# A two-layer hybrid mixer step: the running sum of its branches kept in DRAM, low weight parts made from SBUF, and four conditioning chunks moved into attention

## The chip, the cores and the metric

The kernel runs on one core of one Trainium2 chip. The metric is device time in microseconds (us). TensorE (PE) multiplies, VectorE (DVE) and ScalarE (ACT) work element by element, GpSimd (POOL) does some elementwise work and issues the DMAs that add to what is already at their destination, and SyncE (SP) issues most other DMAs. Each engine runs its own queue of instructions in order and waits on semaphores.

## The reference, cut to what matters

Two layers work on 128 context tokens and 512 latent tokens, 640 in all, with a model width of 1024 in float32. Each layer is

```python
def trunk_layer(x, cond, p, latent, k_ctx, v_ctx):
    mod = jax.nn.silu(cond) @ p['w_ada'] + p['b_ada']
    shift, scale, gate = jnp.split(mod, 3, axis=-1)
    h = rms_norm(x, p['norm_g']) * (1.0 + scale) + shift
    y, k, v = parallel_mixer(h, p, latent, k_ctx, v_ctx)
    return x + gate * y, k, v

    # parallel_mixer: u = h @ p['w_in'] (1024 x 11264), then four branches of u:
    ya = (conformer_conv(...) * jax.nn.silu(a_gate)) @ p['wo_conv']
    yb = (hyena(...) * jax.nn.silu(b_gate)) @ p['wo_hyena']
    yc = (multiscale_pool(...) * jax.nn.silu(c_gate)) @ p['wo_pool']
    yd = (attention(...) * jax.nn.silu(d_gate)) @ p['wo_attn']
    gm = jax.nn.sigmoid(g_merge).reshape(B, L, N_BRANCH, D_MODEL)
    merged = gm[:, :, 0] * ya + gm[:, :, 1] * yb + gm[:, :, 2] * yc + gm[:, :, 3] * yd
    return merged @ p['w_out'], k, v
```

## The kernel before

**Products in three passes.** To keep float32 accuracy with the fast fp32r matmul, every operand is split into a high part and a low part, and each product is high times high, low activation times high weight, and high activation times low weight. `weights()` prepares one weight tile of 128 x 1024: SP loads it as `raw`, ACT casts it to `whi`, ACT writes minus `whi` into `wlo`, and POOL issues a DMA that reads the same weight from DRAM a second time and adds it to `wlo`. (Before the variable `pooled` is set, DVE subtracts instead.) There are two `raw` buffers and three pairs of `whi` and `wlo`. In a tile's 48 matmuls of 320 columns the 16 with `whi` come before the 8 with `wlo`, once for each half (320 tokens) of the activations.

**The order of work.** The Python program runs some generators ("threads") under a planner, the class `Loom`, which decides when each thread may put its next matmuls into PE's queue. It knows estimated costs and latencies, but not when a DMA lands. PE runs exactly that order. The other engines' queues are ordered by a scheduler, with a head start for `weights()`.

**Memory.** Large tiles live in 13 slots of 128 x 2632 floats. Smaller rings hold tiles `t` (3), `u` (4) and `k` (4).

**One layer.** `layers()` does the input projections for Hyena, the attention, and then four calls of `merge()`, one for each branch, each with eight output blocks `d`: a gate projection into the tile `th`, the branch's output projection, and `th` times it. The first call (Hyena) stores `th` in DRAM (`mscr`). `reload()` brings all eight blocks back into two slots (`merged`) during the attention; the calls for attention and pool ("mid") add `th` there with DVE, and the last one (conv) adds and splits the sum. `out_proj()` multiplies with `w_out`, adds the residual, and lets `turned()` (transposes) and `modulated()` (norm, scale, split) make the next layer's input, the two halves of tokens one after the other.

**Conditioning.** `ada_chunk()` multiplies a chunk of `w_ada` (1024 x 256) with the two conditioning vectors: two loads of 512 KB into a `whi` and a `wlo` buffer, 8 matmuls of 256 columns, one copy on ACT (`k<-ax`), and for a gate chunk a store to `grow`. There are 24 chunks: 8 for the first layer at the start, 12 spread over its first stages with a pause of 14 us, and the last 4, the second layer's gates, at lowest priority while the first layer's `out_proj` runs.

**Hyena's tables.** `tables()` loads 1.25 MB into a slot; the second layer's filters are made during the first layer's pool stage, their spectra are kept in DRAM, and the table's slot stays occupied until the second layer's Hyena is done.

Of the kernel before, what the change touches and what calls it, by code (L numbers as in the profile page):

```python
# [10 lines left out]
F32R = mybir.dt.float32r  # L11
# [14 lines left out]
    0, 1024, 1536, 3072, 3584, 4096, 4608, 5632, 5888, 6144, 7168)  # L26
R_DW, R_DWB, R_LNG, R_LNB, R_SW, R_SB, R_SK, R_PS, R_NG, R_BA, NROW = 0, 31, 32, 33, 34, 43, 46, 48, 49, 51, 55
SLOT = 2632
NSLOT = 13
NRAW = 2  # L30
NHI = 3
DORD = "0f4xt15gh2637"
PT = 6.5
# [1 line left out]
HW = 80  # L35
HA = 40
PL = 1
GS = 40.0
EACH = 0.003
ORD = "01456237vkq"  # L40
WAHEAD = 120
# [191 lines left out]
def hybrid_flow_backbone(ctx: ExitStack, tc: tile.TileContext, i, o):  # L233
# [49 lines left out]
    def slot(dt=F32):  # L283
        yield lambda: 0.0 if free else INF
        return Slot(dt)
# [47 lines left out]
    def weights(src, kk, n):  # L333
        yield from wr.get()
        lm.bg = True
        with tc.high_priority(offset=WAHEAD):
            raw = wp.tile([P, 1024], F32, tag="raw", name=nm("raw"), bufs=NRAW)
            hi = wp.tile([P, 1024], F32R, tag="whi", name=nm("whi"), bufs=NHI)
            lo = wp.tile([P, 1024], F32R, tag="wlo", name=nm("wlo"), bufs=NHI)
            w = kk * n  # L340
            rv = raw[:, 0:w]
            sp.dma_start(out=rv.rearrange("p (k c) -> p k c", k=kk), in_=src)
            act.copy(hi[:, 0:w], rv)
            if pooled[0]:

                act.activation(out=lo[:, 0:w], in_=r32(hi[:, 0:w]), func=AF.Copy, scale=-1.0)
                nc.gpsimd.dma_start(out=lo[:, 0:w].rearrange("p (k c) -> p k c", k=kk), in_=src.bitcast(F32R),  # L347
                                    accum_op=ALU.add)
            else:
                dve.tensor_tensor(out=lo[:, 0:w], in0=rv, in1=r32(hi[:, 0:w]), op=ALU.subtract)  # L350
        lm.bg = False
        return (hi[:, 0:w].rearrange("p (k c) -> p k c", k=kk),
                lo[:, 0:w].rearrange("p (k c) -> p k c", k=kk))
# [355 lines left out]
    def ada_later(jobs, step, start):  # L709
        yield lm.pe + start  # L710
        for l, j in jobs:
            yield from ada_chunk(l, j)
            if 4 <= j < 8:
                ada_finish(l, j - 4)
            yield lm.pe + step
# [130 lines left out]
        tr.put()  # L846


    def merge(l, b, ga, nk, wo, merged, mode, ma=None, wait=None):


        for d in range(8):
            if mode == "last" and d % 4 == 0:
                for part in (ma.hi, ma.lo):
                    part.append((yield from slot(F32R)))
            th = yield from tr.get(T)

            def gate(j, ps):
                act.activation(out=th[:, 320 * j:320 * j + 320], in_=ps, func=AF.Tanh, scale=0.5)

            yield from in_proj(l, C_GM + b * D + 128 * d, gate)
            if wait is not None:
                yield wait
            w = yield from weights(wo[:, 128 * d:128 * d + 128].rearrange("(k p) c -> p k c", p=P), nk, 128)
            def take(j, ps):
                tj = th[:, 320 * j:320 * j + 320]
                dve.scalar_tensor_tensor(out=tj, in0=tj, scalar=1.0, in1=ps, op0=ALU.add, op1=ALU.mult)

            yield from both(w, 0, ga, nk, take)
            wr.put(WD)  # L870
            if mode == "first":
                sp.dma_start(out=mscr[l, d], in_=th)
                lm.cur.t += 2.5
            else:
                yield lambda: 0.0 if len(merged) == 2 else INF
                mv = merged[d // 4].v((d % 4) * T, T)
                dve.tensor_tensor(out=mv, in0=mv, in1=th, op=ALU.add)
                if mode == "last":
                    split(ma.h(d), ma.l(d), mv, 0.5)
            tr.put()  # L880

    hT = [None]
# [3 lines left out]
    class Hyena:  # L886
# [32 lines left out]
        def filters(self, q):  # L919
# [115 lines left out]
            if self.nf == 2:  # L1035
                self.Bf.free()
                if early:
                    self.fs.free()
                    self.flt = {}

        def spectra(self):

            yield lambda: 0.0 if self.nf == 2 else INF
            for c in range(4):
                yield lambda: 0.0 if c < 2 or c in self.bu else INF
                self.flt[c] = yield from slot()
                for q in range(2):
                    self.ev_f[c, q].t = load(self.flt[c].v(1280 * q, 1280), spec[c, q])
# [178 lines left out]
    class Attention:  # L1227
        def __init__(self, l):
            self.l = l
            self.gD = [None, None]  # L1230
            self.sT, self.qT, self.rq, self.qv, self.den = {}, {}, {}, {}, {}
            self.ev_kv, self.ev_s, self.ev_v, self.ev_room, self.ev_gd = (Event(lm) for _ in range(5))
            self.ev_q = [Event(lm) for _ in range(4)]
            self.ev_p = [Event(lm) for _ in range(4)]
            self.nq = [0] * 4
            self.nk = 0
            self.hi, self.lo = [], []
            self.pairs, self.ev_pair = [], []
# [359 lines left out]
        def parts(self):  # L1598

            yield self.ev_s  # L1600
            for c in range(8):
                if c % 4 == 0:
                    self.hi.append((yield from slot(F32R)))
                    self.lo.append((yield from slot(F32R)))
                if c == 4:
                    self.ev_room.set()
                yield self.done[c]
                split(self.hi[c // 4].v((c % 4) * T, T), self.lo[c // 4].v((c % 4) * T, T),
                      self.gD[c // 4].v((c % 4) * T, T), 0.5)
# [281 lines left out]
    def layers():  # L1891
# [3 lines left out]
        for l in range(DEPTH):  # L1895
# [37 lines left out]
            lm.spawn(at.values_out(), 0, LATV)  # L1933
            lm.spawn(at.run(), 5.5)
            lm.spawn(at.parts(), 4)
            yield hy.ev_done
            yield from merge(l, 1, hy.gb, 4, i["wo_hyena"][l], None, "first")
            hy.gb.free()
            cv = Conv(l)
            cv.at = at  # L1940
            yield from cv.inputs(range(4))

            merged = []
            lm.spawn(reload(l, merged, at.ev_room), 5)
            gd = Act(at.hi, at.lo)
            lm.spawn(cv.taps(), -1)
            po = Pooling(l)
# [1 line left out]
            po.at = at  # L1949
            lm.spawn(po.windows(), -3)  # L1950
            lm.spawn(cv.norm(), -2, LATN)
            yield from merge(l, 3, gd, 8, i["wo_attn"][l], merged, "mid", None, at.ev_gd)
            gd.free()

            yield from po.gated()
            if l + 1 < DEPTH:
                hys[l + 1].after = cv.ev_norm
                for q in range(2):
                    lm.spawn(hys[l + 1].filters(q), PF0 + q / 10)
            yield from merge(l, 2, po.pa, 4, i["wo_pool"][l], merged, "mid")  # L1960
            po.pa.free()

            yield from cv.gated()
            ma = Act([], [])
            rows = yield from gate_rows(l)
            yield from merge(l, 0, cv.ga, 4, i["wo_conv"][l], merged, "last", ma)
            cv.ga.free()
            hT[0].free()
            for s in merged:
                s.free()  # L1970
            xs = yield from slots(2)
            if l == 0:
                load_x(xs, i["x_prompt"][0], i["x_sample"][0])
            else:
                load_x(xs, scratch[0:LP], scratch[LP:T])
            ssq = sm.tile([P, 5, 4], F32, tag="ssq", name=nm("ssq"))
            if l + 1 < DEPTH:
                lm.spawn(ada_later([(1, j) for j in range(8, 12)], 0.0, GS), 50, LATA)
            if l + 1 < DEPTH:
                xT = yield from slots(2)  # L1980
                evs = [[Event(lm) for _ in range(2)] for _ in range(4)]
# [12 lines left out]
                for x in xs:  # L1994
                    x.free()

    def reload(l, merged, ev):

        yield ev
        for h in range(2):  # L2000
            s = yield from slot()
            load(s.v(0, 4, T), mscr[l, 4 * h:4 * h + 4].rearrange("d p t -> p d t"))
            merged.append(s)

    ev_prm, ev_cond, ev_ssq = Event(lm), Event(lm), Event(lm)
    ev_hdn = [Event(lm) for _ in range(DEPTH)]
    ev_mod = [[Event(lm) for _ in range(4)] for _ in range(DEPTH)]
# [9 lines left out]
    t_hid, t_prm = [0.0], [0.0]  # L2017
    small = load_hidden(s_hid) + [(sel, i["c_sel"], t_prm)] + load_params(s_prm) + [(edge, i["c_edge"], t_prm)]
    chunks = []
    spare = ["whi", "wlo"] * 3 + ["raw"] * 2  # L2020
    h0 = hys[0]
    xs0 = [Slot(), Slot()]

# [138 lines left out]
```

## Time and profile before

| | us |
|---|---|
| median of the runs shown (3) | 2272.85 |
| their lowest and highest | 2267.57, 2273.87 |
| time of the profiled execution | 2271.39 |
| its span, first to last instruction | 2269.6 |
| PE busy in the span | 2189.7 |
| DVE, ACT, POOL busy in the span | 1329.2, 1190.8, 585.5 |

1.8 us of the profiled execution lie outside its span. The profile gives the clock that TensorE was granted as a share of full speed; its mean is 0.992 here. Matmuls are pipelined, so the durations of neighbouring rows overlap, and a stretch's speed is read from start to start.

### The profile page before, as it was taken

The page shows a single profiled execution, that of the slowest core. Times are in us where ns is not written, and L with a number is a line of the kernel's source. Part 1 is how long each engine was busy: PE and PEld are TensorE (multiplying, and loading weights), DVE is VectorE, ACT ScalarE, POOL GpSimd, SP SyncE. Part 2 cuts the span into 40 slices and gives each one's busy share as a digit, 9 for nine tenths or more (in the row PEclk, how much of TensorE's full clock was granted, in tenths as well). Part 3 has the DMA queues.
Part 4 walks back from the last instruction along what each step waited for, and adds up shares of the span by engine and source line. Part 5 has one row for each costly group of instructions (what it writes and reads, how often), then busy time and mean ns, then how long its engine had stood idle before and what let it go on. Part 6 is the DMA issues. An engine that isn't in the chain of part 4 may idle for free. (4 is left out here: it accounts for less than half of the span.)

```text
span 2269.6 us, 40007 instructions
## 1 busy us (share of the span) xinstructions
PE 2189.7 (96%) x15951; PEld 2140.5 (94%) x15951; DVE 1329.2 (59%) x2791; ACT 1190.8 (52%) x2179; POOL 585.5 (26%) x451
## 2 busy tenths in 40 slices
PE   5999999999999999999997999999999999999999
PEld 3899999999999998999996999999999999999999
DVE  5676786656679945443224677855764899612222
ACT  5544457667664345444445544656676543544442
POOL 1744321111012222554211333111111122222221
PEclk9899999999999999999998999999999999999999
DMA  8476775545568879778898865555466698698986
GB/s 277 110 156 137 156 159 114 97 95 99 106 122 147 149 126 182 154 164 161 150 220 239 154 118 120 110 102 101 84 110 118 126 155 150 120 162 148 174 171 138
DMA packets 510536, 322.33 MB, mean 142 GB/s; under 512 B 13016, under 2 KB 499608, under 8 KB 510093
## 3 DMA queue, kind: packets, MB, share of 16 engines
q0 software_dynamic: 223856, 122.96, 42.7%
q1 hardware_dynamic: 285780, 196.68, 28.6%
q8 instruction: 125, 2.05, 0.4%
q14 instruction: 62, 0.51, 0.1%
q10 hardware_dynamic: 713, 0.14, 0.0%
HBM read 302.26 MB, written 17.47 MB: 141 GB/s over the span
## 5 line engine op out<-in xcount | busy, mean ns | idle before, releaser
L193 PE MATMUL mm<-sl,whi 128*128 128x320 f32 x6304 | 1059.1, 313 | 10.6 <-DVE t L178 3.2
L193 PEld LDWEIGHTS mm<-sl,whi 128*128 128x128 f32 x6304 | 951.2, 189 | 18.2 <-DVE sl L178 4.3
L193 PE MATMUL mm<-sl,wlo 128*128 128x320 f32 x3152 | 555.1, 312 | 5.7 <-DMA wlo<-in_w_in_dram 5.7
L347 POOL DMA_DIRECT2D wlo<-in_w_in_dram x173 | 264.4, 1532 | 915.6 <-ACT wlo L178 689.5
L193 PEld LDWEIGHTS mm<-sl,wlo 128*128 128x128 f32 x3152 | 484.0, 189 | 7.4 <-DMA wlo<-in_w_in_dram 6.7
L178 ACT CAST whi<-raw 128x1024 fp32r<-128x1024 f32 (+2 forms) x272 | 255.3, 939 | 429.4 <-PE mm L193 405.1
L178 ACT ACTIVATE wlo<-whi 128x1024 fp32r<-128x1024 f32 (+2 forms) x269 | 254.9, 948 | 29.6 <-PE mm L193 25.7
L178 DVE SCALAR_TENSOR_TENSOR t<-t,mm 128x320 f32<-128x320 f32 x192 | 93.0, 485 | 294.1 <-PE mm L193 244.4
L193 PE MATMUL mm<-whi,sl 128*128 128x256 f32 x1600 | 226.2, 284 | 2.5 <-ACT u L178 1.5
L178 DVE SCALAR_TENSOR_TENSOR sc<-sl,prm,sc 128x640 f32<-128x640 f32 (+14 forms) x232 | 207.3, 893 | 11.4 <-ACT sc L178 6.7
L193 PE MATMUL sc<-sl,sl 128*128 128x128 f32 (+1 forms) x1344 | 203.4, 293 | 5.7 <-DVE u L178 2.8
L193 PEld LDWEIGHTS mm<-whi,sl 128*128 128x128 f32 x1600 | 203.3, 188 | 4.8 <-ACT u L178 1.7
L178 DVE TENSOR_TENSOR h<-ax,h 128x512 fp32r<-128x512 f32 (+1 forms) x200 | 120.1, 604 | 118.7 <-ACT h L178 117.5
L193 PEld LDWEIGHTS sc<-sl,sl 128*128 128x128 f32 x1344 | 179.5, 194 | 8.0 <-DVE u L178 4.0
L178 ACT ACTIVATE t<-mm 128x320 f32<-128x320 f32 x208 | 90.0, 433 | 137.8 <-PE mm L193 135.1
L178 DVE TENSOR_SCALAR_CACHE_REDUCE u<-sc,rq 128x640 f32<-128x640 f32 x128 | 112.6, 880 | 46.2 <-PE sc L193 45.2
L178 ACT ACTIVATE u<-u,nb 128x640 f32<-128x640 f32 x128 | 106.2, 830 | 52.3 <-DVE u L178 51.6
L178 ACT CAST h<-ax 128x512 fp32r<-128x512 f32 (+1 forms) x200 | 102.5, 515 | 55.8 <-PE ax L202 53.6
L193 PE MATMUL mm<-wlo,sl 128*128 128x256 f32 x800 | 126.7, 281 | 4.4 <-DMA wlo<-in_w_in_dram 4.4
L193 PE MATMUL ax<-h,sl 128*128 128x256 f32 (+1 forms) x656 | 120.7, 295 | 4.0 <-DVE h L178 2.7
L202 PE MATMUL ax<-ident,u 128*128 128x128 f32 x752 | 118.5, 273 | 4.7 <-DVE h L178 2.6
L193 PEld LDWEIGHTS mm<-wlo,sl 128*128 128x128 f32 x800 | 108.3, 188 | 5.0 <-DMA wlo<-in_w_in_dram 5.0
(211 smaller groups left out, 2225.9 us busy)
## 6 DMA issues: line engine op xcount, KB each, us to landing
raw<-in_w_in_dram SPq DMA_DIRECT2D x176, 512.0 KB
wlo<-in_w_in_dram POOLq DMA_DIRECT2D x173, 512.0 KB, 6.6
wlo<-in_w_ada_dram SPq DMA_DIRECT2D x19, 512.0 KB
whi<-in_w_ada_dram SPq DMA_DIRECT2D x19, 512.0 KB
raw<-in_wo_attn_dram SPq DMA_DIRECT2D x16, 512.0 KB
wlo<-in_wo_attn_dram POOLq DMA_DIRECT2D x16, 512.0 KB, 6.4
raw<-in_w_out_dram SPq DMA_DIRECT2D x16, 512.0 KB
wlo<-in_w_out_dram POOLq DMA_DIRECT2D x16, 512.0 KB, 6.0
```

The lines of the kernel that those rows point to most:

```text
L178: r = f(*args, **kw)
L193: r = self.real.matmul(out, lhsT, rhs, **kw)
L202: r = self.real.transpose(out, in_, ident)
L347: nc.gpsimd.dma_start(out=lo[:, 0:w].rearrange("p (k c) -> p k c", k=kk), in_=src.bitcast(F32R), accum_op=ALU.add)
```

## The change

- In `weights()`, the DMA that adds to `wlo` reads the tile `raw` in SBUF and not the weight in DRAM: 128 runs of up to 4 KB where it had up to 1024 runs of 512 B. `raw` is thus in use until that DMA has landed, and there are four `raw` buffers.
- There are 12 slots and not 13.
- The two "mid" merges add `th` to `mscr` in DRAM by a DMA on POOL's queue (32 DMAs of 320 KB in all). `reload()` and its two slots are gone; the last merge loads one block of the sum at a time into a tile `u` (16 loads of 320 KB on SP's queue).
- The second layer's four gate chunks run in its own attention, with the pause of 14 us, and not at the end of the first layer.
- Hyena's table slot is freed when the second layer's filters are made, and the table is loaded again at the start of the second layer.
- At the start, two more of the first chunks' halves go to `raw` buffers.

```diff
-NSLOT = 13
-NRAW = 2
+NSLOT = 12
+NRAW = 4
...
                 act.activation(out=lo[:, 0:w], in_=r32(hi[:, 0:w]), func=AF.Copy, scale=-1.0)
-                nc.gpsimd.dma_start(out=lo[:, 0:w].rearrange("p (k c) -> p k c", k=kk), in_=src.bitcast(F32R),
-                                    accum_op=ALU.add)
+                nc.gpsimd.dma_start(out=r32(lo[:, 0:w]), in_=rv, accum_op=ALU.add)
...
+            if mode == "last":
+                mv = yield from ur.get(T)
+                now = load(mv, mscr[l, d])
             th = yield from tr.get(T)
...
             if mode == "first":
                 sp.dma_start(out=mscr[l, d], in_=th)
                 lm.cur.t += 2.5
+            elif mode == "mid":
+                nc.gpsimd.dma_start(out=mscr[l, d], in_=th, accum_op=ALU.add)
+                lm.cur.t += 5.0
             else:
-                yield lambda: 0.0 if len(merged) == 2 else INF
-                mv = merged[d // 4].v((d % 4) * T, T)
+                lm.cur.t = max(lm.cur.t, now)
                 dve.tensor_tensor(out=mv, in0=mv, in1=th, op=ALU.add)
-                if mode == "last":
-                    split(ma.h(d), ma.l(d), mv, 0.5)
+                split(ma.h(d), ma.l(d), mv, 0.5)
+                ur.put()
...
                 if early:
                     self.fs.free()
+                    self.tabE.free()
...
             yield lambda: 0.0 if self.nf == 2 else INF
+            self.tables((yield from slot()))
...
             lm.spawn(at.parts(), 4)
+            if l:
+                lm.spawn(ada_later([(1, j) for j in range(8, 12)], ASTEP, 0.0), 5, LATA)
...
-            merged = []
-            lm.spawn(reload(l, merged, at.ev_room), 5)
...
-            if l + 1 < DEPTH:
-                lm.spawn(ada_later([(1, j) for j in range(8, 12)], 0.0, GS), 50, LATA)
...
-    spare = ["whi", "wlo"] * 3 + ["raw"] * 2
+    spare = ["whi", "wlo"] * 3 + ["raw"] * 4
```

The change moves instructions on every engine. Three places matter for what follows.

On PE, the end of the first layer. The rows with `cs` are the gate chunks (`whi` and `wlo` hold halves of `w_ada`), those with `ident` are transposes of the residual, and the last rows are the first matmuls of the second layer's first `w_in` tile. Before:

```order
L193 MATMUL ax_13052<-whi_13035,cs 32x256 x4
L193 MATMUL ax_13052<-wlo_13037,cs 32x256 x4
L202 MATMUL mm_13073<-ident,sl_12254 128x128 x2
L202 MATMUL mm_13077<-ident,sl_12254 128x128 x2
L193 MATMUL ax_13088<-whi_13084,cs 32x256 x4
L193 MATMUL ax_13088<-wlo_13086,cs 32x256 x4
L193 MATMUL ax_13110<-whi_13106,cs 32x256 x4
L193 MATMUL ax_13110<-wlo_13108,cs 32x256 x4
L193 MATMUL mm_13176<-sl_12262,whi_13160 128x320
L193 MATMUL mm_13176<-sl_12264,whi_13160 128x320
```

Now:

```order
L201 MATMUL mm_13038<-ident,sl_12267 128x128 x2
L201 MATMUL ax_13042<-ident,sl_12267 128x128
L201 MATMUL mm_13057<-ident,sl_12267 128x128 x2
L201 MATMUL mm_13061<-ident,sl_12267 128x128 x2
L192 MATMUL mm_13102<-sl_12275,whi_13089 128x320
L192 MATMUL mm_13102<-sl_12277,whi_13089 128x320
```

The four chunks are gone from between the last transposes and the second layer's first matmuls; the other matmuls of this place stand in the same order.

On ACT, the same place. `k<-ax` are the chunks' copies, `sl<-u` makes high parts of the second layer's input, `sl<-mm` and `sl<-ax` read transposes, and `whi<-raw`, `wlo<-whi` prepare `w_in` tiles. Before, the first two tiles of the second layer are prepared together, after the third chunk's place:

```order
L178 ACTIVATE sl_12261<-mm_13025,mod_1705 128x256
L178 COPY k_13081<-ax_13052 128x256
L178 ACTIVATE sl_12261<-ax_13032,mod_1705 128x128
L178 ACTIVATE sl_12262<-u_13039,mod_1705 128x128
L178 ACTIVATE sl_12262<-u_13039,mod_1705 128x192
L178 CAST whi_13160<-raw_13159 128x1024
L178 CAST whi_13170<-raw_13169 128x1024
L178 ACTIVATE wlo_13161<-whi_13160 128x1024
L178 ACTIVATE wlo_13171<-whi_13170 128x1024
L178 ACTIVATE sl_12261<-mm_13045,mod_1705 128x256
```

Now the first tile's low part (`wlo<-whi`) stands ahead of the norm's row (`t<-ax`, 128 x 384) and the second tile's two parts right behind it; `o` are squares of the residual:

```order
L177 ACTIVATE wlo_13090<-whi_13089 128x1024
L177 ACTIVATE o_12794,ssq_12272<-sl_12267 128x256
L177 ACTIVATE o_12852,ssq_12272<-sl_12267 128x256
L177 ACTIVATE o_12906,ssq_12272<-sl_12267 128x256
L177 ACTIVATE o_12908,ssq_12272<-sl_12267 128x256
L177 COPY t_12279<-ax_12959 128x384
L177 CAST whi_13096<-raw_13095 128x1024
L177 ACTIVATE sl_12275<-u_12964,mod_1708 128x128
L177 ACTIVATE wlo_13097<-whi_13096 128x1024
L177 ACTIVATE sl_12275<-u_12964,mod_1708 128x192
```

What moved is the preparation of these two tiles: from the middle of the input's conversion to its beginning.

On SP, the second layer's attention. `whi<-in_w_ada` and `wlo<-in_w_ada` are a gate chunk's loads and `raw` is a weight tile's. Before, the queue holds weight loads and the first merge's stores at this place:

```order
L342 DMA raw_16070<-in_w_in_dram 128x8x128
L872 DMA mscr<-t_15518 128x640
L342 DMA raw_16216<-in_wo_hyena_dram 128x4x128
L342 DMA raw_16278<-in_w_in_dram 128x8x128
L872 DMA mscr<-t_15699 128x640
L342 DMA raw_16416<-in_w_in_dram 128x4x256
```

Now a chunk's two loads stand behind loads of weight tiles, which wait in turn until a `raw` buffer's low part has landed:

```order
L341 DMA raw_15433<-in_w_in_dram 128x8x128
L341 DMA raw_15597<-in_wo_hyena_dram 128x4x128
L656 DMA whi_15238<-in_w_ada_dram 128x4x256
L656 DMA wlo_15240<-in_w_ada_dram 128x4x256
L1350 DMA out_dram<-sl_14812 128x256
L341 DMA raw_15685<-in_w_in_dram 128x8x128
L341 DMA raw_15842<-in_wo_hyena_dram 128x4x128
L341 DMA raw_15904<-in_w_in_dram 128x8x128
L656 DMA whi_15505<-in_w_ada_dram 128x4x256
L656 DMA wlo_15507<-in_w_ada_dram 128x4x256
```

Four such pairs of loads have come into this stretch, in order behind the weights' own.

## Rows read from the trace of the kernel before

**Rows 1.** The page of the whole execution: its span, and TensorE's busy time.

```profile
span 2269.6 us, 40007 instructions
...
PE 2189.7 (96%) x15951; PEld 2140.5 (94%) x15951; DVE 1329.2 (59%) x2791; ACT 1190.8 (52%) x2179; POOL 585.5 (26%) x451
```

**Rows 2.** Who PE waited for, whole span: us in total, times, longest us.

```profile
PE mm L193 <- DMA wlo<-in_w_in_dram: 10.1, 6, 2.9
PE ax L193 <- DMA wlo<-in_w_ada_dram: 7.6, 4, 3.8
PE ax L193 <- DMA whi<-in_w_ada_dram: 1.6, 3, 0.9
```

**Rows 3.** Stretches of 10 us: length, PE busy, granted clock, DMA share, GB/s.

```profile
1200.00:1210.00 10.00, 8.56 (x79) 1.00 0.22 67
1210.00:1220.00 10.00, 5.00 (x62) 0.99 1.01 327
1220.00:1230.00 10.00, 7.30 (x32) 0.67 1.05 230
1230.00:1240.00 10.00, 7.71 (x33) 0.67 1.26 247
1240.00:1250.00 10.00, 9.24 (x58) 0.99 0.77 209
...
2120.00:2130.00 10.00, 10.00 (x70) 1.00 1.11 250
```

**Rows 4.** PE in order of time around the layer boundary; idle before a row in brackets.

```profile
1207.28 1.10 PE L193 MATMUL mm<-wlo,sl 128*128 128x256 f32 x8
...
1209.40 0.64 PE L193 MATMUL ax<-whi,cs 128*32 128x256 f32 x8
...
1209.86 0.61 PE L193 MATMUL ax<-wlo,cs 128*32 128x256 f32 x8
...
1214.17 0.64 PE L193 MATMUL ax<-wlo,cs 128*32 128x256 f32 x8 [2.32 <-DMA wlo<-in_w_ada_dram]
...
1221.04 4.30 PE L193 MATMUL mm<-sl,whi 128*128 128x320 f32 x16
...
1227.92 1.44 PE L193 MATMUL mm<-sl,wlo 128*128 128x320 f32 x4 [2.58 <-DMA wlo<-in_w_in_dram]
...
1236.69 2.41 PE L193 MATMUL mm<-sl,wlo 128*128 128x320 f32 x8 [2.29 <-DMA wlo<-in_w_in_dram]
...
1243.48 1.33 PE L193 MATMUL mm<-sl,wlo 128*128 128x320 f32 x8
```

**Rows 5.** The same boundary on the other engines, in order of time.

```profile
1207.94 0.38 SPq L658 DMA_DIRECT2D wlo<-in_w_ada_dram  x1
...
1214.93 0.37 ACT L178 COPY k<-ax 128x256 f32<-128x256 f32 x1 [2.25 <-PE ax L193]
...
1216.10 1.98 ACT L178 CAST whi<-raw 128x1024 fp32r<-128x1024 f32 x2
...
1217.98 2.00 ACT L178 ACTIVATE wlo<-whi 128x1024 fp32r<-128x1024 f32 x2
...
1219.46 3.14 POOL L347 DMA_DIRECT2D wlo<-in_w_in_dram  x2 [33.09 <-ACT wlo L178]
...
1223.82 1.05 DVE L178 SCALAR_TENSOR_TENSOR sl<-u,mod,sl 128x192 fp32r<-128x192 f32 x3 [0.27 <-ACT sl L178]
```

**Rows 6.** DMA issues: KB each, median us from issue to landing.

```profile
wlo<-in_w_in_dram POOLq DMA_DIRECT2D x173, 512.0 KB, 6.6
...
wlo<-in_pool_w_dram POOLq DMA_DIRECT2D x8, 64.0 KB, 2.6
```

**Rows 7.** The two longest other waits of PE for a low part.

```profile
307.82 0.74 PE L193 MATMUL mm<-wlo,sl 128*128 128x256 f32 x4 [1.21 <-DMA wlo<-in_w_in_dram]
...
1541.65 0.74 PE L193 MATMUL mm<-wlo,sl 128*128 128x256 f32 x4 [2.94 <-DMA wlo<-in_w_in_dram]
```

**Rows 8.** VectorE by form: busy us, mean ns of one; idle before it.

```profile
L178 DVE TENSOR_TENSOR sl<-sl,t 128x640 f32<-128x640 f32 x64 | 53.3, 832 | 1.3
```

More of the change, by code (lines that the diff above doesn't have):

```diff
@@ L37 @@
 PL = 1
-GS = 40.0
 EACH = 0.003
@@ L846, in modulated, with merge @@
         tr.put()
-    def merge(l, b, ga, nk, wo, merged, mode, ma=None, wait=None):
+    def merge(l, b, ga, nk, wo, mode, ma=None, wait=None):
         for d in range(8):
@@ L1231, in __init__ @@
             self.sT, self.qT, self.rq, self.qv, self.den = {}, {}, {}, {}, {}
-            self.ev_kv, self.ev_s, self.ev_v, self.ev_room, self.ev_gd = (Event(lm) for _ in range(5))
+            self.ev_kv, self.ev_s, self.ev_v, self.ev_gd = (Event(lm) for _ in range(4))
             self.ev_q = [Event(lm) for _ in range(4)]
@@ L1604, in parts @@
                     self.lo.append((yield from slot(F32R)))
-                if c == 4:
-                    self.ev_room.set()
                 yield self.done[c]
@@ L1935, in layers @@
             lm.spawn(at.parts(), 4)
+            if l:
+                lm.spawn(ada_later([(1, j) for j in range(8, 12)], ASTEP, 0.0), 5, LATA)
             yield hy.ev_done
-            yield from merge(l, 1, hy.gb, 4, i["wo_hyena"][l], None, "first")
+            yield from merge(l, 1, hy.gb, 4, i["wo_hyena"][l], "first")
             hy.gb.free()
@@ L1951, in layers @@
             lm.spawn(cv.norm(), -2, LATN)
-            yield from merge(l, 3, gd, 8, i["wo_attn"][l], merged, "mid", None, at.ev_gd)
+            yield from merge(l, 3, gd, 8, i["wo_attn"][l], "mid", None, at.ev_gd)
             gd.free()
@@ L1959, in layers @@
                     lm.spawn(hys[l + 1].filters(q), PF0 + q / 10)
-            yield from merge(l, 2, po.pa, 4, i["wo_pool"][l], merged, "mid")
+            yield from merge(l, 2, po.pa, 4, i["wo_pool"][l], "mid")
             po.pa.free()
@@ L1965, in layers @@
             rows = yield from gate_rows(l)
-            yield from merge(l, 0, cv.ga, 4, i["wo_conv"][l], merged, "last", ma)
+            yield from merge(l, 0, cv.ga, 4, i["wo_conv"][l], "last", ma)
             cv.ga.free()
             hT[0].free()
-            for s in merged:
-                s.free()
             xs = yield from slots(2)
@@ L1995, in layers @@
                     x.free()
[L1997 to L2003, printed above, removed]
     ev_prm, ev_cond, ev_ssq = Event(lm), Event(lm), Event(lm)
```

## The prediction

> **What bounds the kernel now.** I read the page first: PE is busy for 2189.7 of 2269.6 us [rows 1]. The matmuls are the same in number and shape after the change, so what can be won lies in the other 79.9 us and in stretches at a low clock; what can be lost is more waits of this kind. The page's busy shares of DVE, ACT and POOL (59%, 52% and 26% [rows 1]) say that none of them is the bound over the whole span, only in places. Then I read who PE waited for. Low parts of `w_in` tiles cost 10.1 us in 6 waits, and loads of conditioning chunks 7.6 and 1.6 us [rows 2]. The reader should see that these are two of the things that the change touches, and that they are small.
>
> Next come stretches of 10 us. From 1200 to 1250 PE is busy for 37.8 of 50 us, and from 1220 to 1240 the granted clock is 0.67, a mixture of the two levels, 2.4 GHz (1.00) and 1.2 GHz (0.50): about 13 of these 20 us were at the lower one. The DMA engines are full there (shares 1.05 and 1.26). In a merge late in the kernel PE has no pause in 10 us, 70 matmuls in 10 us or 143 ns each, with DMA engines just as full (1.11) [rows 3]. So a full DMA does not slow matmuls whose tiles were prepared in time, and the merges have nothing to give.
>
> The order of time at the layer boundary shows why it is slow. `out_proj` ends at 1207.28 + 1.10 = 1208.38. Then PE does the gate chunks, in order, although their loads are not there yet (the wait of 2.32 us is one of them), and the second layer begins at 1221.04. Its low parts come late twice (2.58 and 2.29 us), and the 16 high-part matmuls of the first tile's second half are through at 1243.48 [rows 4]. On the other engines: the chunks sit in the `whi` and `wlo` buffers, so ACT cannot prepare the first two tiles before 1216.10; it does so in the middle of converting the new layer's input (1.98 and 2.00 us), after it has waited 2.25 us for a chunk's matmuls to copy them. POOL had nothing to issue for 33.09 us. The input's first half is ready when DVE ends at 1223.82 + 1.05 = 1224.87 [rows 5].
>
> **The change, part by part.** *The gate chunks leave the boundary.* PE's order there is otherwise the same. I follow the chain that stays: ACT's conversion of the first half. Out of it go one tile's preparation (half of 1.98 + 2.00, so 1.99 us; the other tile's stays in the chain), the wait of 2.25 and three chunk copies of 0.37 [rows 5], 5.35 us together: the first half is ready at 1219.5. The second tile's low part is negated about 2 us after `out_proj` ends, issued in 1.57 (half of 3.14) and landed 6.6 us later even at today's speed [rows 5, 6], at 1218.6, so no low part is awaited. PE then has left: the first tile's last high matmul (1219.8), 8 with its low part, 24 of the second tile, 16 of the second half. At the lower clock level a matmul here took 4.30 / 16 = 0.27 us [rows 4], so 48 of them take 12.9 us: 1232.7 where it was 1243.48, a gain of **10.8 us**. At the full level they take 48 x 0.143 = 6.9 us and the gain is 16.8; if ACT's chain does not shrink, it is 5.4. I take the lower level, since PE was busy for only 5.00 of the 10 us ahead of 1220, and will have less to do there now [rows 3]. The Trainium skill says the same against this change (TensorE: Matmul & The Clock Gate, section HAM oscillation): a wait for data between groups of matmuls throttles the clock, and the next group starts at half speed. The trace agrees with 0.67; by that rule the sum keeps 10.8, without it 16.8.
>
> *They come into the second layer's attention.* A chunk takes PE 1209.86 + 0.61 - 1209.40 = 1.07 us [rows 4], four of them **4.3 us**, where PE mostly has other work. Falling into waits they would cost nothing; waiting for their loads they cost more (below). I take 4.3.
>
> *Low parts from SBUF.* A low part lands 6.6 us after its issue for 512 KB in up to 1024 runs, and 2.6 us for 64 KB in 128 runs [rows 6]. The new DMA has 128 runs and 512 KB. By runs alone it would be 2.6, by bytes 6.6; I take 4, nearer to the runs, because the bytes no longer come from DRAM twice. Besides the boundary, PE lost 10.1 - 2.58 - 2.29 = 5.2 us to low parts [rows 2, 4], the longest waits being 2.94 and 1.21 [rows 7]. With 2.6 us less, 0.3 of the longest stays and the rest goes: **4.9 us** gained, between 0 and 5.2. By the Trainium skill's fit (DMA: Bandwidth & Descriptors, section Anatomy of one DMA) of 2.0 us and the bytes over 436 GB/s, the landing would be 3.2 us, an estimate; the gain would then be 5.2. Today's 6.6 is twice that fit, so the trace does not bear it out for runs of 512 B from DRAM.
>
> *Four raw buffers.* They let SP load two tiles further ahead; PE's waits name low parts, not `raw`, so I count nothing. That `raw` is held until its low part lands delays a reload by about the landing, against a lead of two more tiles of up to 48 matmuls (6.9 us) each.
>
> *The sum in DRAM.* 32 additions of 832 ns [rows 8] leave DVE, on which no merge waits: nothing. POOL gets 32 DMAs more, about 50 us if each takes the 1.57 of a low part's issue; it is busy for 585.5 of 2269.6 us [rows 1]. Behind such a DMA on POOL's queue stands the next tile's low part. It is not needed before the tile's 16 high matmuls (2.3 us), and its ACT work takes 2 us (1.98 + 2.00 for two tiles [rows 5]) after the same matmuls that the DMA waits for: nothing, 2 us at most in all. The last merge's loads wait for additions that were done a stage earlier, and two `u` tiles keep one load ahead: nothing.
>
> *Slots and the table.* The two slots of `reload()` are no longer taken, so 12 are as good as 11 were in attention, but there is one less in the first layer's Hyena. The extra table load of 1.25 MB comes at a time when 4 MB of chunks have left the same queue. The planner has put many branch matmuls into another order in both attentions; no row prices that, and I allow 5 us either way, half of the 10.1 us that PE now loses to low parts in the whole kernel, as a choice.
>
> **Sum**, against the profiled time of 2271.39: 2271.39 - 10.8 - 4.9 + 4.3 = 2260.0. The median of the runs shown is 1.46 above that execution, so the forecast is **2261.5 us**.
>
> **The rivals.** *Chunk loads that come late (slower).* A chunk's two loads now stand behind weight loads on SP's queue, and those wait for a low part to land. At the boundary a load took from 1207.94 to 1214.17, 6.2 us, until its matmuls ran [rows 4, 5]. If every chunk makes PE wait that long, it is 4 x 6.2 = 24.8 us: 2286. It turns the result to slower from 4.6 us each. Against it: in the whole first layer and the start the other 20 chunks cost only what is left of 7.6 + 1.6 us [rows 2], and in the new order 10 to 14 us of matmuls (48 of 320 columns are 6.9 us) lie between the last use of a chunk's buffers and the chunk.
>
> *Low parts land no sooner.* If the addition itself, and not the reading of short runs, sets the 6.6 us, the 4.9 us stay lost: 2266.4, at the border of no change. The Trainium skill has a mechanism (SBUF — State Buffer, section SBUF: two separate sides): a DMA issued by GpSimd cannot get its descriptors written while certain VectorE operations hold the shared port. No row here shows it apart from the 6.6.
>
> *The clock stays up at the boundary.* 6 us more are gained: 2255.5. For it speaks that PE gets work 1.5 us sooner; against it the longer pause.
>
> *The boundary keeps its length*, since ACT, DVE and the norm between them set it and not the chunks: 2261.5 + 5.4 = 2266.9, and with 5 us lost by the new order 2272. Then the change does nothing that a measurement sees.
>
> **How the numbers follow.** Chances: forecast 0.45, late chunk loads 0.16, low parts no sooner 0.17, clock up 0.12, boundary unchanged 0.10. The measurement tells about 0.3%, 6.8 us: faster is below 2266.0, slower above 2279.7. The forecast and the third rival are faster, 0.57. The slow landing and the unchanged boundary make most of "same", 0.25, with a loss by the new order at their upper edge. Slower has the late loads and a bad order, 0.18. The range: at the low end all gains at their best and chunks for nothing, 2271.39 - 16.8 - 5.2 + 1.46 = 2250.9, and 4 us of a better order: 2247. At the high end 2271.39 - 5.4 + 4.3 + 5 + 1.46 = 2276.8: 2277. That leaves most of the late loads outside, and little else. The forecast's own range is 2254 to 2268.
>
> **What would show it.** Right: the second layer's first matmul with `whi` lies 2 to 8 us after `out_proj`, no wait for `wlo` follows, and the point that was 1243.48 - 1208.38 = 35.1 us behind the end of `out_proj` is about 24 us behind it; the clock is low once there; the median landing of `wlo` is near 4 us; PE's waits for `wlo` are below 1 us in total; the chunks appear in the second attention without waits. Wrong: `ax<-in_w_ada` waits in the second attention, new waits in its scores or in the first layer's Hyena, a landing near 6.6, or waits on POOL with `mscr` in front.

## The result and the profile after

| | before | changed |
|---|---|---|
| median, us | 2271.95 (4 runs) | 2322.42 (4 runs) |
| ratio, 95% interval | | 1.0222 (1.0208 to 1.0237) |
| span of the profiled execution, us | 2269.6 | 2319.1 |

The change makes the kernel 50 us slower, where the forecast was 11 us faster and the range ended at 2277. The page of the changed kernel (busy us, share of the span, number of instructions; then the queue on which POOL's DMAs run):

```profile
span 2319.1 us, 40179 instructions
...
PE 2207.8 (95%) x15951; PEld 2158.1 (93%) x15951; DVE 1304.7 (56%) x2759; ACT 1190.4 (51%) x2179; POOL 454.3 (20%) x483
...
q0 software_dynamic: 43760, 133.45, 32.0%
```

PE has the same work and is busy 18 us longer [rows 1], at a mean granted clock of 0.978 (0.992 before); the other 31 us are new pauses. POOL is busy for 131 us less, and its DMAs, with 10 MB more to move, need 43760 packets where they needed 223856. So what the change does with DMAs is cheaper for the engines, and yet the kernel is slower. Who PE waited for (total us, times, longest):

```profile
PE ax L201 <- DVE sl L177: 16.1, 6, 8.8
PE mm L192 <- DVE t L177: 16.0, 9, 5.3
PE sc L192 <- DVE sl L177: 13.7, 3, 5.8
PE sc L192 <- DVE wx L177: 12.4, 3, 6.5
PE ax L192 <- DVE sl L177: 9.0, 7, 2.5
PE ax L192 <- DMA wlo<-in_w_ada_dram: 3.9, 1, 3.9
```

The waits for `wlo` of `w_in` [rows 2] are gone completely, and the chunk of `w_ada` that is still waited for is the one at the start. In their place PE waits for DVE: in Hyena (`sc`, `ax`) and in merges (`mm` waits for DVE to read the last product). Stretches of 10 us show where (length, PE busy, granted clock, DMA share, GB/s):

```profile
160.00:170.00 10.00, 5.81 (x30) 0.72 0.48 119
170.00:180.00 10.00, 6.60 (x54) 0.84 0.52 112
180.00:190.00 10.00, 4.18 (x17) 0.50 0.41 98
190.00:200.00 10.00, 10.00 (x84) 0.91 0.35 107
280.00:290.00 10.00, 5.41 (x38) 0.66 0.65 169
290.00:300.00 10.00, 6.65 (x44) 0.83 0.30 101
1250.00:1260.00 10.00, 6.46 (x47) 1.00 0.44 103
1260.00:1270.00 10.00, 9.01 (x43) 0.66 0.87 266
1270.00:1280.00 10.00, 9.25 (x58) 1.00 0.75 219
```

From 160 to 200 and from 280 to 300 PE stands still and then works at a low clock, while the DMA share is moderate: this is the first layer's Hyena, which the change touches through the number of slots, besides its low parts. The last three rows are the layer boundary, which answers to [rows 3] and did become shorter. PE there in order of time, for comparison with [rows 4]:

```profile
1253.92 1.11 PE L192 MATMUL mm<-wlo,sl 128*128 128x256 f32 x8
...
1261.68 4.64 PE L192 MATMUL mm<-sl,whi 128*128 128x320 f32 x16 [0.56 <-ACT sl L177]
...
1267.87 2.52 PE L192 MATMUL mm<-sl,whi 128*128 128x320 f32 x16
...
1274.81 0.88 PE L192 MATMUL mm<-sl,whi 128*128 128x320 f32 x3 [0.17 <-DVE sl L177]
```

`out_proj` ends at 1253.92 + 1.11 = 1255.03, the second layer's first matmul starts 6.65 us later, without a chunk between, and the first tile's second half is through at 1274.81 + 0.88 = 1275.69, 20.7 us behind `out_proj`. That point was 35.1 us behind it: 14.4 us are won here. The low parts' landings, for [rows 6] (KB each, median us from issue to landing):

```profile
wlo<-raw POOLq DMA_DIRECT2D x205, 512.0 KB, 5.2
...
wlo<-raw POOLq DMA_DIRECT2D x56, 256.0 KB, 4.3
mscr<-t POOLq DMA_DIRECT2D x32, 320.0 KB, 5.2
```

To place the loss in time I count PE's matmuls over stretches of 10 us and compare when the same number is done. Against before at 170 us the changed kernel is some 4 us ahead; at 330 us 24 behind; at 810 us 20; at 1210 us, just ahead of the boundary, 48; at the end 49. So the first Hyena loses some 28 us, the stage from 810 to 1210 us another 28, and the second layer gives back what the boundary wins, most of it in its own Hyena, where PE waits 4.9 and 4.5 us for DVE at 1415 and 1424 us.

### The profile page after: what moved, and what is told of

It is laid out like the page before. It is cut to its first block, busy times and chain, and to the rows that moved or that the text cites. A ratio compares the mean times of both kernels' runs of the same rounds, so it can differ in the third digit from the quotient of the medians.

```text
span 2319.1 us, 40179 instructions
## 1 busy us (share of the span) xinstructions
PE 2207.8 (95%) x15951; PEld 2158.1 (93%) x15951; DVE 1304.7 (56%) x2759; ACT 1190.4 (51%) x2179; POOL 454.3 (20%) x483
## 3 DMA queue, kind: packets, MB, share of 16 engines
q0 software_dynamic: 43760, 133.45, 32.0%
## 4 chain that ended last, share of the span: by engine, by line
PE 81%; DVE 7%; DMA 5%; issue 3%; ACT 2%; POOL 1%; SPq 1%; ACTq 0%; POOLq 0%; DVEq 0%
PE mm L192 64%; PE sc L192 6%; PE ax L192 6%; PE ax L201 4%; DVE sl L177 3%; DMA sl<-in_hy_w_dram 1%; DVE wx L177 1%; SPq L324 1%; DMA wlo<-raw 1%; DMA spec<-sl 1%; DVE k L177 1%; ACT sl L177 1%; ACT k L177 0%; DVE u L177 0%; POOL sl L177 0%
## 5 line engine op out<-in xcount | busy, mean ns | idle before, releaser
L346 POOL DMA_DIRECT2D wlo<-raw x269 | 238.1, 885 | 1536.9 <-ACT wlo L177 1197.8
L192 PE MATMUL sc<-sl,sl 128*128 128x128 f32 (+1 forms) x1344 | 210.7, 301 | 26.3 <-DVE sl L177 13.7
L192 PEld LDWEIGHTS sc<-sl,sl 128*128 128x128 f32 x1344 | 186.9, 201 | 28.7 <-issue 20.6
```

The costliest lines, as they stand in the source:

```text
L192: r = self.real.matmul(out, lhsT, rhs, **kw)
L346: nc.gpsimd.dma_start(out=r32(lo[:, 0:w]), in_=rv, accum_op=ALU.add)
```

## The experiments

Theory S: the lost slot costs the time. Rivals: R, `raw` is held until its low part lands, which stops SP's queue; D, the sum in DRAM; O, the planner's order around the sum. Each run's median stands with its ratio to the kernel before, measured beside it on the same chip, and the ratio's 95% interval.

**Low parts from SBUF alone**, in the kernel before (two raws, 13 slots):

```diff
-                nc.gpsimd.dma_start(out=lo..., in_=src.bitcast(F32R), accum_op=ALU.add)
+                nc.gpsimd.dma_start(out=r32(lo[:, 0:w]), in_=rv, accum_op=ALU.add)
```

> The kernel before with one edit: low parts are added from the tile raw in SBUF, still with two raw buffers and 13 slots; the order of PE's matmuls is that of before. Theory S (the slot that was taken away is what made the change slow): this edit is innocent and a little good, 2272 less 2 to 5 us, 2267 to 2270; PE's waits for wlo in w_in and w_out stages vanish as they did in the changed kernel. Rival R (raw is held until its low part has landed, so that SP's queue stands at the next raw load, and the loads behind it, the filters' hy_w among them, come late): slower than before, 2280 or more, with long waits of ACT for hy_w.

2319.43 us, 1.0203 (1.0183 to 1.0224): R holds where there are two raws. Who ACT waited for:

```profile
ACT whi L178 <- DMA raw<-in_w_in_dram: 250.6, 48, 8.6
...
ACT whi L178 <- DMA raw<-in_w_out_dram: 56.9, 11, 9.3
```

That is 59 waits for `raw` of these two weights, 307.5 us, where three were before (8.3 + 10.6 us). ACT's waits for the filters' `hy_w`, which the rival named as well, hardly grew (19.5 us, 14.0 before). One round of a late merge shows the loop (SP, ACT, POOL):

```profile
2187.42 0.37 SPq L342 DMA_DIRECT2D raw<-in_w_in_dram  x1
...
2191.50 1.05 ACT L178 CAST whi<-raw 128x1024 fp32r<-128x1024 f32 x1 [6.57 <-DMA raw<-in_w_in_dram]
...
2192.58 1.06 ACT L178 ACTIVATE wlo<-whi 128x1024 fp32r<-128x1024 f32 x1
...
2193.94 0.86 POOL L347 DMA_DIRECT2D wlo<-raw  x1 [8.18 <-ACT wlo L178]
...
2198.63 0.37 SPq L342 DMA_DIRECT2D raw<-in_w_in_dram  x1
```

The load issued at 2187.42 is cast at 2191.50, negated at 2192.58, and its addition is issued at 2193.94; the next load into that buffer goes out only at 2198.63, when the addition has landed. The loop takes 11.2 us. PE's 72 matmuls of a round take 10.3 us at 143 ns [rows 3], so the loop sets the pace. With the low part read from DRAM, nothing but the cast reads the buffer.

**The changed kernel with 13 slots**, whose room (10.3 KB per partition) comes from two raws of 4 KB and what was free:

```diff
-NSLOT = 12
-NRAW = 4
+NSLOT = 13
+NRAW = 2
...
-    spare = ["whi", "wlo"] * 3 + ["raw"] * 4
+    spare = ["whi", "wlo"] * 3 + ["raw"] * 2
```

> The changed kernel with 13 slots again; the room for that comes from raw, of which there are two and not four. In work done, the changed kernel lost about 31 us in the first layer's Hyena (160 to 350 us), 24 us between 850 and 1070 us, 10 us in the second layer's Hyena, and won about 9 at the boundary. Theory S: the losses in both Hyenas go away, 2322 less 41 gives 2281; if the losses between 850 and 1070 us come from slots too, 2257. Rival D (the sum in DRAM makes the stage from 850 to 1070 us slow, since th is held until its 5 us addition lands): 2281 and the waits mm<-DVE t there stay. Rival R (raw held): no better than the changed kernel, 2320 or more, since there are fewer raws.

2379.57 us, 1.0458 (1.0429 to 1.0488). Alone it says nothing on the slot: two raws cost more than a slot gives.

**The changed kernel with two and with three raws** (12 slots; the first chunks' halves at the start use two `raw` buffers in both, as in the run above):

```diff
-NRAW = 4
+NRAW = 2    (the first run)
+NRAW = 3    (the second run)
```

> The changed kernel, 12 slots, with two raw buffers in place of four; PE's order is the same but for seven rows at the very start. It separates the raws from the slots in the run with 13 slots. Theory S: the raws matter little, 2317 to 2327. Rival R: two raws held by landing low parts stop SP's queue more often, 2335 or more; if four raws let SP's queue run into buffers that are not free, two of them would make it faster, 2310 or less.

> The changed kernel with three raws; two took 2416, four 2322. PE's order is that of the run with two. If a raw held by its landing low part needs only one more buffer to be hidden (a landing of about 5 us against 6.9 us of matmuls for a tile), 2322 to 2335; if the loads come late whenever one buffer less is there, in the middle, 2355 to 2385.

2416.13 us, 1.0621 (1.0600 to 1.0643) with two; 2324.63 us, 1.0226 (1.0209 to 1.0243) with three, as with four. One buffer more hides the landing, as the first case of the expectation had it: with three, ACT's waits for `raw` of `w_in` come to

```profile
ACT whi L177 <- DMA raw<-in_w_in_dram: 23.7, 6, 5.3
```

Two raws with 13 slots took 2379.57, so with two raws the slot is worth 36.6 us.

**The changed kernel with low parts from DRAM again** (12 slots, four raws, PE's order unchanged; the diff is the first one above, reversed):

> The changed kernel with one edit undone: the addition that makes a low part reads the weight in DRAM again; 12 slots, four raws and PE's order stay those of the changed kernel. With two raws the addition from SBUF cost 46 us by itself in the kernel before, and 94 us lay between two and four raws in the changed kernel. Rival R (also with four raws, raw held until its low part lands is what slows the change): clearly faster than the changed kernel, 2295 or less. Theory S (with four raws the edit does no harm, what is lost comes from the slot and from the sum in DRAM): the waits for wlo come back, 2322 plus 0 to 8 us, 2322 to 2330.

2323.21 us, 1.0215 (1.0200 to 1.0230): R falls for four raws: with them the edit neither costs nor brings anything here. PE waits 11.6 us for low parts of `w_in` in this run and 0 in the changed kernel, at the same time within 1 us.

**Gate chunks alone**, moved into the second attention of the kernel before:

```diff
+            if l:
+                lm.spawn(ada_later([(1, j) for j in range(8, 12)], ASTEP, 0.0), 5, LATA)
...
-            if l + 1 < DEPTH:
-                lm.spawn(ada_later([(1, j) for j in range(8, 12)], 0.0, GS), 50, LATA)
```

> The kernel before with one edit: the four gate chunks are worked in the second layer's attention and not at the boundary. By the recorded sum 2272 less 10.8 and plus 4.3: 2265.5, with the first high-part matmul of layer two 2 to 8 us behind out_proj. If the chunks' loads come late in the attention: 2272 less 10 plus up to 25, 2287. If the new order of attention costs what the planner's filler hid before: 2270 to 2275.

2262.33 us, 0.9952 (0.9936 to 0.9969). It is the fastest kernel of this study, ahead of the kernel before and of the changed one. PE at its boundary:

```profile
1205.02 1.10 PE L193 MATMUL mm<-wlo,sl 128*128 128x256 f32 x8
...
1212.77 4.40 PE L193 MATMUL mm<-sl,whi 128*128 128x320 f32 x16 [0.81 <-ACT sl L178]
...
1221.91 2.08 PE L193 MATMUL mm<-sl,whi 128*128 128x320 f32 x11
...
1225.87 0.42 PE L193 MATMUL mm<-sl,whi 128*128 128x320 f32 x1 [0.16 <-DVE sl L178]
```

`out_proj` ends at 1206.12, the point is at 1226.29, 20.2 us behind: 14.9 us won. Less the 4.3 us of chunks that makes 10.6, and 11.0 were measured.

**The sum in DRAM alone**, and with the gate chunks and the second table load (both with 13 slots, two raws, low parts from DRAM):

```diff
+            elif mode == "mid":
+                nc.gpsimd.dma_start(out=mscr[l, d], in_=th, accum_op=ALU.add)
...
-            lm.spawn(reload(l, merged, at.ev_room), 5)
```

> The kernel before with the running sum in DRAM alone: reload() is gone, the two middle merges add to mscr through POOL's queue, the last loads it block by block. 13 slots, two raws, low parts from DRAM, gate chunks at the boundary, the table kept. Theory D (the sum in DRAM makes the stage of the last merges and of the second layer's filters slow, since th is held until its addition has landed and POOL's queue has more to issue): 2272 plus the 24 us that the changed kernel lost between 850 and 1070, about 2296. If those 24 us come from the lost slot: 2268 to 2277.

> The changed kernel with 13 slots, two raws and low parts from DRAM: so the sum in DRAM, the gate chunks in attention and the table's second load remain. PE's order is that of the run with 13 slots and low parts from SBUF, which took 2379.6. If the parts add up it is the run with the sum in DRAM alone less the 11 us of the gate chunks: theory D 2285, if the sum in DRAM costs nothing 2258 to 2266. Against the changed kernel with low parts from DRAM (12 slots) it prices the slot.

2296.85 us, 1.0103 (1.0088 to 1.0118), and 2279.65 us, 1.0028 (1.0017 to 1.0039). The sum in DRAM costs 22.6 us, as D expected; whether by the ways that D names is looked at below. The chunks and the table's second load gain 17.2 us in this kernel, where the chunks alone gained 11.0 in that of before; no run shows why they gain more. The second run against that with 12 slots (2323.21) prices the slot at 43.6 us, in which two `raw` buffers in place of four are counted in. Against the run with 13 slots, two raws and low parts from SBUF (2379.57) it is 99.9 us faster: there the edit that took 46 us in the kernel before costs twice as much.

**What in the sum costs.** Two slots taken and left empty where `reload()` held them; the additions left out, so that the result lacks the other branches; both:

```diff
+    def reload(l, merged, ev):
+        yield ev
+        for h in range(2):
+            s = yield from slot()
+            merged.append(s)
...
-                nc.gpsimd.dma_start(out=mscr[l, d], in_=th, accum_op=ALU.add)
```

> The run with the sum in DRAM alone (2296.85), but two slots are taken and given back where reload() did, and stay empty. So the additions and loads through DRAM stay, and PE's order comes close to that of before in the first layer (some 60 rows differ there ahead of the last merge, against some 560 without the slots). Theory O (free slots let the planner start the second layer's filters earlier, into the pool and conv merges, where their loads come late; the sum in DRAM itself costs nothing): 2270 to 2279. Theory D (the additions into DRAM, on POOL's queue and by holding th, cost the 24 us): 2290 to 2300.

> The run with the sum in DRAM alone, with the 32 additions into DRAM left out; so the first branch alone comes back in the last merge, and the other branches are missing from the sum. PE's order is the same, row for row. Theory D: the 24 us go away with the additions, 2270 to 2279. Theory O: 2290 to 2298, and the same late hy_w loads on ACT between 970 and 1030 us.

> The run with the sum in DRAM and two slots held (2294.7), with the 32 additions into DRAM left out, so that the other branches are missing from the sum; PE's order is that of that run, row for row. So far: sum in DRAM 2296.9, the same without additions 2286.0, with held slots 2294.7; before 2273.9. If the additions are one cause (their traffic makes low parts and filter loads land later) and the order with freed slots the other, both are gone here: 2272 to 2280. If the additions are worth 11 us and what else is lost is in something that both keep (the loads of the sum in the last merge, the u tiles that they hold, the rest of the order): 2282 to 2287.

2294.70 us, 1.0086 (1.0068 to 1.0104) with held slots; 2285.97 us, 1.0046 (1.0028 to 1.0063) without additions; 2283.96 us, 1.0040 (1.0024 to 1.0055) with held slots and without additions. O falls: holding the slots changes 2 us. The additions are worth 10.9 us in the one order and 10.7 in the other. The remaining 9 us are in something else that the edit brings. What the additions do is seen in the landings from 860 to 1060 us, first with them and then without (KB each, median us):

```profile
wlo<-in_w_in_dram POOLq DMA_DIRECT2D x14, 512.0 KB, 9.3
...
mscr<-t POOLq DMA_DIRECT2D x8, 320.0 KB, 7.4
```

```profile
wlo<-in_w_in_dram POOLq DMA_DIRECT2D x15, 512.0 KB, 7.7
```

With 8 additions in these 200 us a low part lands in 9.3 us, and without them in 7.7. They also hold SP's queue. Who SP's queue waited for from 890 to 950 us, with the additions:

```profile
SPq L324 <- DMA mscr<-t: 15.3, 2, 8.1
```

The last merge's first two loads of the sum stand there, in the middle of the merge before, and wait for its additions, with weight loads behind them; they go out at 913.91 and 923.64, and without the additions both at 887.49. Two other ways fall by the same traces. A low part is issued by POOL 0.7 us behind ACT's negation on average with the additions and 0.6 without (850 to 1090 us), so POOL's queue is not the way; and the waits for a tile `t` that a DMA into `mscr` still reads come to 0.7 us in the whole run. How the 10.9 us divide between longer landings and SP's queue is not shown.

Loads of filters (`hy_w`) are late too. In the run with held slots (ACT, ACT, PE):

```profile
1005.45 1.14 ACT L177 CAST k<-sl 64x256 fp32r<-64x256 f32 x3 [10.48 <-DMA sl<-in_hy_w_dram]
...
1006.61 0.44 ACT L177 ACTIVATE t<-mm 128x320 f32<-128x320 f32 x1
...
1006.64 0.58 PE L192 MATMUL ax<-k,hd 128*128 128x256 f32 x1 [9.05 <-ACT k L177]
```

ACT stands 10.48 us at a cast that waits for such a load, and PE waits 9.05 us for its result. The load was issued at 995.62 and was there 9.8 us later; in the kernel before, where ACT waited for them, these loads took 3.0 to 5.4 us from issue to cast. In the changed kernel the same wait reaches a merge (ACT, ACT, DVE, PE):

```profile
1060.72 1.25 ACT L177 CAST k<-sl 64x256 fp32r<-64x256 f32 x3 [6.37 <-DMA sl<-in_hy_w_dram]
1061.88 0.43 ACT L177 ACTIVATE t<-mm 128x320 f32<-128x320 f32 x1
...
1062.40 0.48 DVE L177 SCALAR_TENSOR_TENSOR t<-t,mm 128x320 f32<-128x320 f32 x1
...
1062.94 0.64 PE L192 MATMUL mm<-sl,whi 128*128 128x320 f32 x1 [5.33 <-DVE t L177]
```

ACT waits 6.37 us for the filter's load. Behind that cast stands its copy of a merge's product (`t<-mm`), and behind that DVE's addition of a product, which frees the tile of PSUM (the memory that PE writes its products to) that PE needs: PE waits 5.33 us. One late load of 64 KB stops all three engines. Here it was late by its issue and not by its landing: it was issued at 1055.51, 1.2 us after ACT had fallen idle, and took 5.2 us; SP's loads had stood for the store of the filter before (`spec`), 24.6 us in all from 850 to 1070 us, 12.9 before. And this form is not the sum's alone: PE's waits for `t` in merges come to 16.0 us in the changed kernel and to 12.9 in the next run, which has the order for 12 slots too, but to 1.9 us with the sum in DRAM and 13 slots. No run has that order without the sum.

**The order for 12 slots in a memory of 13** (low parts from DRAM, two raws):

```diff
+NSLOT = 13
...
-        yield lambda: 0.0 if free else INF
+        yield lambda: 0.0 if len(free) > 1 else INF
```

> The changed kernel with low parts from DRAM and two raws, in PE's order of 12 slots, but with 13 slots in memory: the planner still uses 12 at a time, and they rotate, so that a slot has longer to be free before it is written again. With 12 in memory and in the order it took 2323, with 13 in both 2280. If the slot's price is that of real waits for a slot that is still read (a filter's load waited for DVE until 156 us and ACT for that load for 10 us): 2285 to 2300. If the price lies in the planner's order for 12 slots, whatever the memory: 2315 to 2325.

2312.79 us, 1.0171 (1.0155 to 1.0187), between the two expectations and nearer to the order's. With 13 in both it took 2279.65, and the program differs from that one by the last line shown alone; so the order makes 33.1 of the 43.6 us; memory and raws together 10.4. In the first Hyena it is the order alone; PE's pauses there in this run:

```profile
180.85 0.58 PE L192 MATMUL sc<-sl,sl 128*128 128x128 f32 x1 [4.97 <-DVE sl L177]
...
276.12 4.10 PE L192 MATMUL sc<-sl,sl 128*128 128x128 f32 x20 [7.05 <-DVE wx L177]
...
285.40 2.01 PE L192 MATMUL sc<-sl,sl 128*128 128x128 f32 x12 [3.25 <-DVE sl L177]
```

and in the changed kernel:

```profile
186.51 0.80 PE L192 MATMUL sc<-sl,sl 128*128 128x128 f32 x2 [5.82 <-DVE sl L177]
...
276.73 0.83 PE L192 MATMUL mm<-sl,wlo 128*128 128x320 f32 x4
284.10 3.99 PE L192 MATMUL sc<-sl,sl 128*128 128x128 f32 x20 [6.53 <-DVE wx L177]
...
293.37 0.80 PE L192 MATMUL sc<-sl,sl 128*128 128x128 f32 x5 [3.35 <-DVE sl L177]
```

The same groups of transforms (`sc<-sl,sl`) wait for DVE, 4.97, 7.05 and 3.25 us there, 5.82, 6.53 and 3.35 us here, whether the memory has 12 slots or 13. In the changed kernel PE ends four matmuls with a low part at 276.73 + 0.83 = 277.56, and the next rows in its queue are the transforms, for which DVE isn't ready until 284.10: no projection stands between. In the kernel before, at the same stage:

```profile
272.62 2.40 PE L193 MATMUL sc<-sl,sl 128*128 128x128 f32 x20
274.77 1.19 PE L193 MATMUL mm<-whi,sl 128*128 128x256 f32 x8
275.80 0.63 PE L193 MATMUL mm<-wlo,sl 128*128 128x256 f32 x4
...
283.38 2.40 PE L193 MATMUL sc<-sl,sl 128*128 128x128 f32 x20
```

Sixty matmuls of projections of 256 columns stand between these two groups of transforms, and PE has no pause. In this stage such projections begin at 266.95 there, and in the changed kernel only at 296.95, behind the groups that wait. In the run with 13 slots in both, PE's waits for this `sl` of DVE from 140 to 360 us are one of 2.31 and one of 0.75.

## Why the prediction was wrong

The gains were forecast in the right places. **The boundary** went as described: 6.65 us between `out_proj` and the first matmul (2 to 8 forecast), no wait for a low part behind it, one stretch with a clock of 0.66, and a gain of 14.4 us where the sum had 10.8 and the bounds 5.4 to 16.8. The chain came out: the first tile's 16 high matmuls end 11.3 us behind `out_proj`, where the sum had 11.4 (1219.8 less 1208.38). What was mis-sized is the clock behind them: the 48 matmuls counted at the lower level at 12.9 us took 9.4. The first 16 last 4.64 us, the second tile's 16, which start at 1267.87, last 2.52. By the Trainium skill's rule (TensorE: Matmul & The Clock Gate, section HAM oscillation), which the prediction weighed, the group behind the waits starts at half speed; the 4.64 us agree, for that group. **The chunks in attention** cost their 4.3 us and no more; the rival of late chunk loads fell, since no wait for `w_ada` appears in the second attention. **Clock at the boundary** and **boundary unchanged** fell too, the former only halfway.

**Low parts from SBUF**: the step "the rest goes: 4.9 us gained" failed in its second half. The landing came down from 6.6 to 5.2 us, not to 4, and PE's waits for low parts did go to zero; but with them back the kernel was no slower (2323.21 against 2322.42). The 5 us were counted as if nothing stood behind them; here other waits did. The Trainium skill's fit (DMA: Bandwidth & Descriptors, section Anatomy of one DMA) would give an estimate of 3.2 us for this landing; the trace's 5.2 does not bear it out.

**Four raw buffers** at nothing was right for four and for three, by the lead that the prediction named. It missed that this makes the raws part of the low parts' price: with two of them the edit costs 46 us in the kernel before and 99.9 in the changed one with 13 slots.

**The sum in DRAM** is the first failed step: "nothing, 2 us at most in all", and measured 22.6. The prediction looked for the cost on POOL's queue and on DVE and put it at nothing there; for POOL's queue the traces agree. It didn't look at the DMA engines in the one stage in which merges, filter loads and weight loads run together. There the 8 additions of 320 KB lengthen other landings, and those have waiters. And its sentence that the last merge's loads "wait for additions that were done a stage earlier" does not hold: the first two hold SP's queue for 15.3 us in the run with the sum in DRAM alone. Some 11 us of the price are shown to be the additions; for the other 9 the freed slots and the additions are excluded. In the run with held slots and without additions, one wait of 5.0 us for a filter is left, and the rest lies in small pieces which no experiment here separates.

**Slots** are the step that decided. That "there is one less in the first layer's Hyena" was seen and given no price; the "5 us either way" were for another order in the attentions, "as a choice", taken from a row on low parts that had nothing to do with slots. Measured were 43.6, and 33.1 of them are the planner's order alone. The changed order of PE was there to be read ahead of the run: in it groups of transforms that depend on DVE stand one behind the other with almost no projections between. What such a group then waits, 3 to 7 us each, and the low clock behind it are the price in Hyena: PE's waits from 140 to 360 us come to 29.1 us, and to 7.7 before.

The terms measured one by one, 22.6 for the sum, -17.2 for gates and table in that kernel, 43.6 for the slot and -0.8 for the low parts with four raws, make 48.2 of the 50.5 us. They are the steps of one chain of kernels, so they add up by themselves, and the 2.3 us left are the kernel before, which took 2274.30 beside the chain's first run and 2271.95 beside the changed kernel.

## What to carry to other kernels

Where a planner fills PE's waits with other work, a buffer is worth the waits that this work covers: read from its new order what stands between a group and the result it depends on, and price what stands uncovered by the producer's chain. A DMA that moves work off an engine had its price here in the busiest stage, on the landings of other loads there and on the queue of a load that waits for it; ask which in-order engine stands at such a load and what queues behind it. And hold a source buffer until a DMA has landed only if there is a buffer more than the loop needs: here two cost 46 to 100 us and three nothing.

## What the runs showed of the hardware

In the changed kernel an addition of 512 KB from SBUF into SBUF in 128 runs lands in 5.2 us (median), of 256 KB in 4.3, and one of 320 KB from SBUF into DRAM in 5.2; the same 512 KB in runs of 512 B from DRAM took 6.6 [rows 6]. So an eighth of the runs, and no second reading from DRAM, saved a fifth of the time. The issue on POOL got much shorter, from 1.57 us to 0.86 (the row at 2193.94 in the run with low parts from SBUF).
